# S5 input products with u as the weights, two groups side by side, and their results transposed back on TensorE

## The chip, the cores and the metric

The kernel runs on one core of a Trainium2 chip, in one launch. Its time is the device time of that core in microseconds, from the runtime; a profiled execution also gives a span, from the first to the last instruction. Five engines run their own instruction streams in order and wait for each other through semaphores: TensorE (PE; its weight loads are listed as PEld), VectorE (DVE), ScalarE (ACT), GpSimd (POOL) and SyncE (SP, which here only issues transfers). SBUF is the on-chip memory, PSUM the eight banks in which PE leaves its results, each 128 partitions of 512 float32.

## The reference

One encoder layer on 512 positions of 1024 features. The normalised input is projected once; the parts feed an S5 state-space branch, a gMLP branch and two gates; then come cross-attention on 256 memory tokens and a SwiGLU. What the change touches is the input side of the S5 scan:

```python
u = xa.astype(f32).reshape(bsz, seq, S5_GROUPS, S5_GROUP).transpose(1, 0, 2, 3)   # 32 groups of 16
lam_bar = jnp.exp(lam * step)
b_bar = ((lam_bar - 1.0) / lam)[..., None] * b
bu = jnp.einsum('gpc,lbgc->lbgp', b_bar, u.astype(jnp.complex64))     # 64 complex states a group
_, states = lax.associative_scan(_linear_recurrence, (a, bu), axis=0, reverse=reverse)
```

The scan runs in both directions over 512 positions.

## The kernel before

The kernel is one long program for the tile framework, whose scheduler sets the order of each engine's instructions, apart from those that the source pins with `in_order`. PE's main work is the layer's matrix products in three passes of float32r halves (`mm3`, L374): weights are loaded (`wraw`), split into `whi` by ACT (L85) and `wlo` by DVE (L86), and multiplied. `tokm` puts four token tiles in four PSUM banks (`pt`); `feat` takes two banks at a time (`pf`). Those banks come from a pool of five (`bank`, tag "mm"); a second pool of three banks (`aux`) serves transposes and small products.

The S5 branch is a generator beside that work. `tick` calls it after each block of products, and `later(n, f)` puts a step n blocks further down the program, so that its products stand between those of `pt` and `pf`. The positions are cut in 64 chunks of 8, and the scan goes over chunks. For each octet o of 8 groups (4 octets) and each of the real and the imaginary part i, so eight times:

- DVE forms 128x1024 coefficients in `wsx` (L972 to L976).
- `turn` transposes them on PE, four in each of two banks `pw` (L951), and ACT copies each bank to its half of the tile `wt` (L952).
- `apply` multiplies: for each group g, the weights are `wt[:, g]`, 128x128, the moving operand is `u[:, g]`, 64 chunks, and the result is 128 partitions (two directions of 64 states) by 64 chunks of the bank `pz` (L958).
- `keep` copies the lower half of the partitions on ACT (L963) and the upper one, reversed in time, on DVE (L964) to `zh`, which the scan (L985 to L988) goes over in place.

In the same stage ACT evacuates `pt` (L1089, `zt`), forms the squares of the gMLP's layer norm (L500, `squares`) from a mean `nm` that DVE made (L1134), normalises `zt` (L1142) with a root `r` from POOL (L1140), and from the first `pf` on evacuates gates (L1175, `gas`, with a table load ahead of the first). Much later, `s5_outputs` multiplies on the output side (L1014, `py`) with the same form that the change uses: weights `ss` or `u` of 64 columns, moving 128 columns, and two column halves j of PE in turn; then copies (`yn`, L1023) and transposes (`pyt`, L1029). For octets 2 and 3 the operand `tt` is loaded from POOL (L926) and the coefficients `e` are reloaded from SP.

Of the kernel before, what the change touches and what calls it, by code (L numbers as in the profile page):

```python
# [9 lines left out]
F32 = mybir.dt.float32  # L10
# [7 lines left out]
P = 128  # L18
# [22 lines left out]
NCH = T // Q  # L41
NO = 4
GO = G // NO
# [9 lines left out]
def hybrid_layer_kernel(  # L53
# [8 lines left out]
    nc = tc.nc  # L62
# [14 lines left out]
    def bank(name):  # L77
        return pm.tile([P, 512], F32, tag="mm", name=name)

    def aux(name, shape=(P, 512)):  # L80
        return pa.tile(list(shape), F32, tag="aux", name=name)
# [12 lines left out]
    in_order = tc.keep_in_program_order  # L94
# [362 lines left out]
    def later(n, fn):  # L457

        side["later"].append((side["now"] + n, fn))
# [30 lines left out]
    ident = cp.tile([P, P], F32, name="ident")  # L490
# [74 lines left out]
    s5p = s5.enter_context(tc.tile_pool(name="s5", bufs=1))  # L565
# [273 lines left out]
    def inner(t, gs, n):  # L839

        return t[:, gs, :].unsqueeze(3).to_broadcast([P, GO, t.shape[2], n])

    def outer(t, gs, n):

        return t[:, gs, :].unsqueeze(2).to_broadcast([P, GO, n, t.shape[2]])

    def lc(t, g):
        return t[:, g].rearrange("p a b -> p (a b)")
# [89 lines left out]
    def s5_inputs(o):  # L938

        gs = slice(o * GO, (o + 1) * GO)  # L940
        br, bi = st["b"]
        pr, pi = st["pw"]
        zh, u = st["zh"], st["u"]

        def turn(i, e):
            turned.add((o, i))
            wt = s5p.tile([P, GO, P], F32, tag="wt", name="wt", bufs=2)
            for hf in range(2):
                ps = aux("pw", (P, 4, P))
                for j in range(4):  # L950
                    nc.tensor.transpose(ps[:, j, :], lc(e, 4 * hf + j), ident)  # L951
                nc.scalar.copy(wt[:, 4 * hf:4 * hf + 4, :], ps)  # L952
            later(0.5, lambda: apply(i, wt))

        def apply(i, wt):
            ps = aux("pz", (P, GO, NCH))
            for g in range(GO):
                nc.tensor.matmul(ps[:, g, :], wt[:, g, :], u[:, o * GO + g, :], start=True, stop=True)  # L958
            zv = zh[:, :, i, gs].rearrange("p n g -> p g n")
            later(0.5, lambda: keep(zv, ps))  # L960

        def keep(zv, ps):
            nc.scalar.copy(zv[lo_], ps[lo_])  # L963
            V.tensor_copy(zv[hi_], ps[hi_, :, ::-1])  # L964
            st["nz"] = st.get("nz", 0) + 1

        for i in range(2):
            while o > 0 and (o - 1, i) not in turned:
                yield None
            e = wsx[:, 2 + i].rearrange("p g (c l) -> p g c l", c=C)  # L970
            w = s5p.tile([P, GO, C, Q], F32, tag="etmp", name="etmp2")
            V.tensor_tensor(e, inner(br, gs, Q), outer((pr, pi)[i], gs, C), ALU.mult)  # L972
            yield 1.1
            V.tensor_tensor(w, inner(bi, gs, Q), outer((pi, pr)[i], gs, C), ALU.mult)
            yield 1.1
            V.tensor_tensor(e, e, w, (ALU.subtract, ALU.add)[i])  # L976
            yield 1.1
            later(1, lambda i=i, e=e: turn(i, e))
# [134 lines left out]
    u = s5p.tile([P, G, NCH], F32, tag="u", name="u")  # L1113
# [74 lines left out]
    for h in range(H):  # L1188
        ps = bank("psv")
# [103 lines left out]
    for q, ts in ((5, T1), (6, T0)):  # L1293
        for i in range(2):
            k = slice(2 * i, 2 * i + 2)
# [308 lines left out]
    ps = {t: bank(f"pt{t}") for t in range(NT)}  # L1604
# [45 lines left out]
    held, ps = [], {}  # L1650
# [91 lines left out]
    ps = [bank("pf0"), bank("pf1")]  # L1742
# [247 lines left out]
```

## Time and profile before

| | us |
|---|---|
| median of 3 runs | 867.08 (866.55 to 867.7) |
| profiled execution | 867.03 |
| its span | 865.2 |
| PE busy in it | 856.6 |
| DVE busy | 660.4 |
| ACT busy | 466.1 |
| first and last start of the input products (L958) | 81.3 and 141.7 |

A row of an engine's timeline gives the start in the span, the length of a run of like instructions, the engine, the source line, the operation, out<-in, sizes and their number; in square brackets stands how long the engine was idle before it and who ended that. A float32 product leaves two MATMUL records, a float32 transpose or a float32r product one. A row of the waits names who waited, for whom, and gives the total in us, the number of times and the longest. A row of the stretches gives the bounds, the length, the busy time with the number of instructions of PE, PEld, DVE, ACT and POOL, the granted PE clock (1.00 is full), the busy share of the DMA engines and GB/s.

### The profile page before, as it was taken

To read this page: it belongs to the slowest core of one execution; us is meant where nothing else is said; L and a number is where in the kernel's file an instruction comes from. 1 tells how busy PE (TensorE), PEld (TensorE's weight loads), DVE (VectorE), ACT (ScalarE), POOL (GpSimd) and SP (SyncE) were. 2 spreads that over 40 slices of the span, in tenths; PEclk is the share of its full clock that TensorE was granted. 3 is DMA by queue.
4 is the path that set the end of the run, shared out by engine and by line. 5 is a ranking of instruction groups with operands and counts; after the bars stand their busy time and mean duration, and the time that the engine had idled before them with its cause. 6 is when DMAs were issued, how large, how long until landed. Compare 5 with 4: busy or idle time off the path is not lost.

```text
span 865.2 us, 14764 instructions
## 1 busy us (share of the span) xinstructions
PE 856.6 (99%) x5780; PEld 766.9 (89%) x5780; DVE 660.4 (76%) x1075; ACT 466.1 (54%) x698; POOL 91.6 (11%) x123
## 2 busy tenths in 40 slices
PE   9999999999999999999999999999999999999997
PEld 7888888888889988899899888999999999988875
DVE  7698997899846868678758756867877768899875
ACT  6734863244355544457547544645545555656564
POOL 0002302111021110110010001010211111000010
PEclk9999999999999999999999999999999999999999
DMA  8759565988574797735696555557899898366672
GB/s 271 192 173 308 110 178 153 252 194 193 145 220 152 242 316 246 238 106 200 210 278 159 144 150 142 146 162 193 206 227 240 217 236 214 96 186 205 197 237 102
DMA packets 115496, 169.56 MB, mean 196 GB/s; under 512 B 9297, under 2 KB 80481, under 8 KB 115298
## 3 DMA queue, kind: packets, MB, share of 16 engines
q1 hardware_dynamic: 94754, 138.50, 48.9%
q0 software_dynamic: 20384, 29.60, 20.5%
q8 instruction: 45, 0.74, 0.3%
q10 hardware_dynamic: 288, 0.52, 0.2%
q14 instruction: 25, 0.20, 0.1%
HBM read 159.71 MB, written 48.73 MB: 241 GB/s over the span
## 4 chain that ended last, share of the span: by engine, by line
PE 95%; DMA 1%; DVE 1%; ACT 1%; issue 1%; POOL 0%; SPq 0%; DVEq 0%; ACTq 0%; POOLq 0%
PE pf L374 27%; PE pt L374 17%; PE px L1238 13%; PE pq L1238 6%; PE dx L374 5%; PE dq L374 3%; PE pv L1238 3%; PE bx L1238 3%; PE qx L1238 3%; PE dv L374 2%; PE pz L958 2%; PE qv L1238 1%; PE po L374 1%; PE psc L374 1%; PE py L1014 1%; PE qq L1238 1%
## 5 line engine op out<-in xcount | busy, mean ns | idle before, releaser
L85 ACT CAST whi<-wraw 128x1024 fp32r<-128x1024 f32 x141 | 145.3, 1030 | 163.0 <-PE pf L374 55.5
L86 DVE TENSOR_TENSOR wlo<-wraw,whi 128x1024 fp32r<-128x1024 f32 x141 | 168.3, 1196 | 64.9 <-ACT whi L85 64.3
L374 PE MATMUL pf<-xn,whi 128*128 128x512 f32 x448 | 140.2, 393 | 0.0
L374 PEld LDWEIGHTS pf<-xn,whi 128*128 128x128 f32 x448 | 83.5, 188 | 16.8
L374 PE MATMUL pf<-xn,wlo 128*128 128x512 f32 x224 | 87.6, 391 | 0.0
L1238 PE MATMUL px<-fn,whi 128*128 128x256 f32 x480 | 83.4, 277 | 0.0
L1238 PEld LDWEIGHTS px<-fn,whi 128*128 128x128 f32 x480 | 72.5, 188 | 0.2
L86 DVE TENSOR_TENSOR wlo<-b,whi 128x1024 fp32r<-128x1024 f32 x40 | 48.9, 1224 | 26.0 <-ACT whi L85 26.0
L85 ACT CAST whi<-b 128x1024 fp32r<-128x1024 f32 x40 | 42.2, 1054 | 48.3 <-PE px L1238 27.8
L1238 PE MATMUL px<-fn,wlo 128*128 128x256 f32 x240 | 66.6, 277 | 0.0
L1238 PE MATMUL pq<-s,whi 128*128 128x256 f32 x320 | 55.0, 277 | 0.0
L374 PE MATMUL dx<-whi,s 128*128 128x512 f32 x166 | 52.2, 391 | 0.4 <-DVE h L1916 0.4
L86 DVE TENSOR_TENSOR wlo<-t,whi 128x1024 fp32r<-128x1024 f32 x30 | 36.7, 1225 | 18.4 <-ACT whi L85 18.4
L85 ACT CAST whi<-t 128x1024 fp32r<-128x1024 f32 x30 | 31.6, 1054 | 34.6 <-PE pv L1238 11.4
L374 PEld LDWEIGHTS pf<-xn,wlo 128*128 128x128 f32 x224 | 42.1, 188 | 8.6
L1238 PEld LDWEIGHTS pq<-s,whi 128*128 128x128 f32 x320 | 48.2, 188 | 0.0
L1238 PEld LDWEIGHTS px<-fn,wlo 128*128 128x128 f32 x240 | 45.2, 188 | 0.0
L1238 PE MATMUL pq<-s,wlo 128*128 128x256 f32 x160 | 44.3, 277 | 0.0
L374 PE MATMUL pt<-whi,xn 128*128 128x512 f32 x128 | 43.1, 403 | 0.0
L374 PEld LDWEIGHTS dx<-whi,s 128*128 128x128 f32 x166 | 31.1, 188 | 7.3 <-issue 0.8
L374 PE MATMUL dx<-wlo,s 128*128 128x512 f32 x83 | 32.3, 391 | 0.6 <-DVE wlo L86 0.6
L289 POOL DMA_DIRECT2D dsum<-in_w_down_dram x12 | 13.3, 1106 | 172.9 <-DMA dsum<-in_w_down_dram 169.2
(458 smaller groups left out, 2225.8 us busy)
## 6 DMA issues: line engine op xcount, KB each, us to landing
wraw<-in_w_in_dram SPq DMA_DIRECT2D x34, 512.0 KB, 4.0
dsum<-in_w_down_dram SPq DMA_DIRECT2D x20, 512.0 KB, 5.5
wraw<-dsum SPq DMA_DIRECT2D x20, 512.0 KB, 4.1
b<-in_w_gate_dram SPq DMA_DIRECT2D x15, 512.0 KB, 5.3
b<-in_w_up_dram SPq DMA_DIRECT2D x15, 512.0 KB, 4.6
wraw<-in_w_down_dram SPq DMA_DIRECT2D x15, 512.0 KB, 3.7
dsum<-in_w_down_dram POOLq DMA_DIRECT2D x10, 512.0 KB, 7.5
dsum<-dsum POOLq DMA_DIRECT2D x10, 512.0 KB, 7.7
```

The lines of the kernel that those rows point to most:

```text
L85: hi = nc.scalar.copy(dst_hi, src)
L86: lo = nc.vector.tensor_tensor(dst_lo, src, dst_hi.bitcast(F32), ALU.subtract)
L289: plan[j + step][1].append((0, lambda d=dst, x=more: nc.gpsimd.dma_start(d, x, accum_op=ALU.add)))
L374: m = nc.tensor.matmul(ps, a[x], b[y], start=start and i == 0, stop=stop and i == 2, skip_group_check=free)
L958: nc.tensor.matmul(ps[:, g, :], wt[:, g, :], u[:, o * GO + g, :], start=True, stop=True)
L1014: in_order(nc.tensor.matmul(ps[64 * j:64 * j + 64, :, :, h, :].rearrange("p q d c -> p d q c"), a, b, start=k == ks[0], stop=k == ks[2], t ...
L1238: nc.tensor.matmul(ps[:, j, :], a[x], b[y], start=start and j == k == i == 0, stop=k == 3 and i == 2, skip_group_check=True)
```

## The change

In `apply` operands change sides. `u[:, g]` (64 columns) is now the stationary weight and `wt[:, g]` (128 columns) moves. Groups 2k and 2k+1 go to the two 64-column halves of PE, so to partitions 0 to 63 and 64 to 127 of the same 128 columns of a bank; the eight products are pinned in that order. The result has chunks on partitions and states along the bank, so ACT copies the bank to `zr` in SBUF, which has one buffer (tag "y" of the pool "s5"), and four transposes of 128x128 bring it back to the layout of before in a bank `pzt`, from which `keep` copies as it did. The products' bank now comes from the pool of five, that of the transposes from the pool of three, where `pz` was before.

```diff
         def apply(i, wt):
-            ps = aux("pz", (P, GO, NCH))
-            for g in range(GO):
-                nc.tensor.matmul(ps[:, g, :], wt[:, g, :], u[:, o * GO + g, :], start=True, stop=True)
+            ps = bank("pz").rearrange("p (k n) -> p k n", k=4)
+            for k in range(4):
+                for j in range(2):
+                    g = 2 * k + j
+                    m = nc.tensor.matmul(ps[64 * j:64 * j + 64, k, :], u[:, o * GO + g, :], wt[:, g, :], start=True,
+                                         stop=True, tile_position=(0, 64 * j))
+                    if g:
+                        in_order(m)
+            zr = s5p.tile([P, 4, P], F32, tag="y", name="zr")
+            nc.scalar.copy(zr, ps)
+            ps = aux("pzt", (P, GO, NCH))
+            for k in range(4):
+                nc.tensor.transpose(ps[:, 2 * k:2 * k + 2, :].rearrange("p g n -> p (g n)"), zr[:, k, :], ident)
             zv = zh[:, :, i, gs].rearrange("p n g -> p g n")
             later(0.5, lambda: keep(zv, ps))
```

The scheduler orders the stage anew; source lines behind the change are 10 higher. The numbers behind names are those of the tile. PE's order where the second group's products stand (o = 0, i = 1), before:

```order
L374 MATMUL pf0_1040<-xn_137,whi_903 128x512
L374 MATMUL pf0_1040<-xn_138,whi_903 128x512
L374 MATMUL pf0_1040<-xn_137,wlo_904 128x512
L951 MATMUL pw_982<-ident_95,wsx_336 128x128 x4
L951 MATMUL pw_988<-ident_95,wsx_336 128x128 x4
L958 MATMUL pz_994<-u_549,wt_950 128x64 x8
```

The tile `wt_950` is copied from pw_951 and pw_957, which stand 25 products of `pt` and `pf` further up, directly behind pz_927. PE's order in the same place now, directly behind the last product of `pt`:

```order
L968 MATMUL pzt_938<-ident_95,zr_936 128x128 x4
L951 MATMUL pw_958<-ident_95,wsx_336 128x128 x4
L951 MATMUL pw_964<-ident_95,wsx_336 128x128 x4
L951 MATMUL pw_989<-ident_95,wsx_336 128x128 x4
L960 MATMUL pz_1001<-wt_957,u_549 64x128 x4
L951 MATMUL pw_995<-ident_95,wsx_336 128x128 x4
L960 MATMUL pz_1001<-wt_957,u_549 64x128 x4
L960 MATMUL pz_1033<-wt_988,u_549 64x128 x4
L374 MATMUL pf0_1061<-xn_137,whi_903 128x512
```

The transposes of two tiles and the products that use them have moved together, and pw_989 takes the PSUM bank of pw_958. ACT's order from the copy of the first group's result on, before:

```order
L963 COPY zh_835<-pz_927 64x8x64
L500 ACTIVATE squares_1032,ss_1088<-zt_334,nm_1087 128x512 x2
L952 COPY wt_950<-pw_951 128x512
L952 COPY wt_950<-pw_957 128x512
L500 ACTIVATE squares_1032,ss_1136<-zt_334,nm_1135 128x512 x2
L1089 ACTIVATE zt_334,zsum_335<-pt2_789 128x512
L85 COPY whi_910<-wraw_901 128x1024
L1089 ACTIVATE zt_334,zsum_335<-pt3_790 128x512
```

And now:

```order
L965 COPY zr_936<-pz_927 128x512
L500 ACTIVATE squares_1053,ss_1109<-zt_334,nm_1108 128x512 x2
L500 ACTIVATE squares_1053,ss_1157<-zt_334,nm_1156 128x512 x2
L1099 ACTIVATE zt_334,zsum_335<-pt2_789 128x512
L85 COPY whi_910<-wraw_901 128x1024
L1099 ACTIVATE zt_334,zsum_335<-pt3_790 128x512
L85 COPY whi_1065<-wraw_908 128x1024
L973 COPY zh_835<-pzt_938 64x8x64
L1152 ACTIVATE zt_334<-zt_334,nm_1108,r_1111 128x1024
L952 COPY wt_957<-pw_958 128x512
L952 COPY wt_957<-pw_964 128x512
```

The two `wt` copies stood behind three instructions of this stretch and now stand behind eleven. Further on, ACT's queue ahead of wt_1093, on which the products pz_1169 wait, is now:

```order
L1152 ACTIVATE zt_334<-zt_334,nm_1256,r_1259 128x1024
L1152 ACTIVATE zt_334<-zt_334,nm_1352,r_1355 128x1024
L85 COPY whi_1128<-wraw_1063 128x1024
L965 COPY zr_1042<-pz_1033 128x512
L973 COPY zh_835<-pzt_1012 64x8x64
L1185 ACT_TABLE_LOAD
L1185 ACTIVATE gas_1217<-pf0_1061 128x512
L85 COPY whi_1228<-wraw_1126 128x1024
L1185 ACTIVATE gas_1220<-pf1_1062 128x512
L973 COPY zh_835<-pzt_1044 64x8x64
L952 COPY wt_1093<-pw_1094 128x512
```

In the densest place (o = 2), PE's order was

```order
L951 MATMUL pw_1171<-ident_95,wsx_336 128x128 x4
L951 MATMUL pw_1177<-ident_95,wsx_336 128x128 x4
L958 MATMUL pz_1243<-u_549,wt_1157 128x64 x8
L374 MATMUL pf0_1195<-xn_137,whi_1107 128x512
L374 MATMUL pf0_1195<-xn_138,whi_1107 128x512
```

and is now

```order
L951 MATMUL pw_1199<-ident_95,wsx_336 128x128 x4
L960 MATMUL pz_1271<-wt_1185,u_549 64x128 x4
L951 MATMUL pw_1205<-ident_95,wsx_336 128x128 x4
L960 MATMUL pz_1271<-wt_1185,u_549 64x128 x4
L960 MATMUL pz_1287<-wt_1198,u_549 64x128 x8
L968 MATMUL pzt_1282<-ident_95,zr_1280 128x128 x4
L968 MATMUL pzt_1298<-ident_95,zr_1296 128x128 x4
L951 MATMUL pw_1304<-ident_95,wsx_336 128x128 x4
L951 MATMUL pw_1310<-ident_95,wsx_336 128x128 x4
L960 MATMUL pz_1369<-wt_1303,u_549 64x128 x4
```

Three groups' steps stand in a row without a product of `pf` between them; pw_1310 takes the bank of pw_1304.

## The prediction

> **What bounds the kernel now.** I read the page's busy shares and its chain first, then what TensorE (PE) waited for, then the stage that the change touches, 75 to 145 us into the span, engine by engine.
>
> ```profile
> span 865.2 us, 14764 instructions
> PE 856.6 (99%) x5780; PEld 766.9 (89%) x5780; DVE 660.4 (76%) x1075; ACT 466.1 (54%) x698; POOL 91.6 (11%) x123
> PE 95%; DMA 1%; DVE 1%; ACT 1%; issue 1%; POOL 0%; SPq 0%; DVEq 0%; ACTq 0%; POOLq 0%
> ```
> ```profile
> PE pt L573 <- DVE ones L493: 1.1, 1, 1.1
> PE dx L374 <- DVE wlo L86: 0.6, 1, 0.6
> ```
> ```profile
> 80.00:90.00 10.00, 10.00 (x59) 8.68 (x58) 9.94 (x15) 6.58 (x16) 2.35 (x2) 1.00 1.04 261
> ```
>
> PE is busy nearly throughout and carries 95% of the chain that ends last; the two longest entries of what it waited for are 1.1 and 0.6 us, at the two ends of the program. In the touched stage PE runs without a gap beside a VectorE (DVE) that is full as well (9.94 of 10 us). So time that PE is spared shows in the result one to one, and so does each new wait of PE. The profiled execution took 867.03 us, 1.8 outside its span; the median of the three runs is 867.08, so nothing has to be shifted.
>
> **The change on PE.** A group of eight input products, and the S5 output products, which already have the form that the change gives to the input products: 128x64 weights, 128 moving columns, two column halves in turn.
>
> ```profile
> 81.27 0.39 PE L374 MATMUL pt<-wlo,xn 128*128 128x512 f32 x1
> 81.50 1.89 PE L958 MATMUL pz<-u,wt 128*128 128x64 f32 x16
> 83.23 1.04 PE L951 MATMUL pw<-ident,wsx 128*128 128x128 f32 x8
> 84.03 0.71 PE L374 MATMUL pt<-whi,xn 128*128 128x512 f32 x2
> 84.57 0.40 PE L374 MATMUL pt<-wlo,xn 128*128 128x512 f32 x1
> 84.81 0.62 PE L374 MATMUL pt<-whi,xn 128*128 128x512 f32 x2
> 85.27 0.39 PE L374 MATMUL pt<-wlo,xn 128*128 128x512 f32 x1
> 89.12 0.62 PE L374 MATMUL pf<-xn,whi 128*128 128x512 f32 x2
> ```
> ```profile
> 240.38 0.39 PE L374 MATMUL pf<-xn,whi 128*128 128x512 f32 x1
> 240.70 0.66 PE L1014 MATMUL py<-e,ss 128*64 128x128 f32 x8
> 241.18 0.39 PE L1014 MATMUL py<-tt,u 128*64 128x128 f32 x4
> 241.40 0.61 PE L1014 MATMUL py<-e,ss 128*64 128x128 f32 x8
> 259.38 0.61 PE L1014 MATMUL py<-e,ss 128*64 128x128 f32 x8
> 259.92 0.39 PE L1238 MATMUL bx<-yb_hi,whi 128*128 128x256 f32 x1
> ```
>
> An operation's length overlaps the next one's; what it costs PE is the step from start to start. A float32 product leaves two records.
> - Removed: eight groups of 16 records, 83.23 - 81.50 = 1.73 us each: 13.8.
> - Added products: the same 16 records at the pace of py (241.40 - 241.18 = 0.22 for four, 0.055 each): 0.88 a group, 7.0 in all.
> - Added transposes: eight take 84.03 - 83.23 = 0.80, so 0.10 each; 32 of them: 3.2.
> - Going into and out of the 64-column form: 240.38 to 240.70 is 0.32 where a step of that row's form is 0.23 (81.27 to 81.50), so 0.09; at the other end eight records from 259.38 at 0.055 end at 259.82 and the next operation starts at 259.92, so 0.10. The order has the products in 12 unbroken pieces: 12 x 0.19 = 2.3.
> - The first float32r product behind float32 work: 84.03 to 84.57 is 0.54 against 0.46 (84.81 to 85.27). There are three more such returns: 0.25.
>
> Sum: -13.8 + 7.0 + 3.2 + 2.3 + 0.25 = -1.05, say -1.0 us. Bounds: without the piece costs -3.4; if the two halves did not run beside each other (then the pace of py would have to differ from its own row), +7 more.
>
> [...]
>
> **The change on ScalarE (ACT).** It gains a copy zr of 128x512 per group, and the two copies of pz (one on ACT, one on DVE) now wait for the transposes. ACT works strictly in its order, and the weight copies (wt from pw) that PE needs next stand behind these. Steps of ACT, start to start, and the DVE and POOL rows that feed it:
>
> ```profile
> 79.24 1.23 DVE L862 TENSOR_TENSOR e<-raw_c,pe 128x1024 f32<-128x1024 f32 x1 [1.96 <-DMA ed<-e]
> 85.00 0.15 DVE L1134 TENSOR_SCALAR nm<-nm 128x1 f32<-128x1 f32 x1
> 86.26 0.15 DVE L1134 TENSOR_SCALAR nm<-nm 128x1 f32<-128x1 f32 x1
> ```
> ```profile
> 85.18 0.72 ACT L500 ACTIVATE squares<-zt,nm 128x512 f32<-128x512 f32 x1 [0.67 <-DVE nm L1134]
> ...
> 85.90 0.71 ACT L500 ACTIVATE squares<-zt,nm 128x512 f32<-128x512 f32 x1
> ...
> 88.97 0.59 ACT L1089 ACTIVATE zt<-pt 128x512 f32<-128x512 f32 x1
> ...
> 89.54 1.04 ACT L85 CAST whi<-wraw 128x1024 fp32r<-128x1024 f32 x1
> 90.48 0.59 ACT L1089 ACTIVATE zt<-pt 128x512 f32<-128x512 f32 x1
> ...
> 93.82 1.24 ACT L1142 ACTIVATE zt<-zt,nm,r 128x1024 f32<-128x1024 f32 x1 [0.74 <-DVE nm L1141]
> 94.97 1.06 ACT L963 COPY zh<-pz 64x512 f32<-64x512 f32 x1
> ...
> 105.72 1.28 ACT L1175 ACT_TABLE_LOAD   x1
> 107.02 0.60 ACT L1175 ACTIVATE gas<-pf 128x512 f32<-128x512 f32 x1
> 107.51 1.04 ACT L85 CAST whi<-wraw 128x1024 fp32r<-128x1024 f32 x1
> ...
> 110.07 1.06 ACT L963 COPY zh<-pz 64x512 f32<-64x512 f32 x1
> 110.92 1.11 ACT L952 COPY wt<-pw 128x512 f32<-128x512 f32 x2
> ```
> ```profile
> 101.77 1.40 POOL L1140 TENSOR_TENSOR r<-ms,mhalf 128x1 f32<-128x1 f32 x1 [7.71 <-DVE ms L1139]
> ```
>
> Steps: squares 0.72, evacuation zt 0.57, cast 0.94, normalisation 1.15, zh 0.85, gate gas 0.49, table load 1.30. Two wt copies take 1.11, so a 128x512 copy about 0.6, with 0.5 to the next one.
>
> *First wait.* Until the first group nothing differs, so the clock of before holds. PE: products 81.50 + 0.09 + 0.88 = 82.47; then the 22 products of pt, which before took 84.03 to 89.12, 5.09: with the exit they end at 87.66; pzt and two pw, 12 transposes: 88.9. Next stands pw_989, whose PSUM bank is that of pw_958, so it waits for that tile's wt copy; behind it the products of pz need the same copy. ACT: zr 82.7; the squares need nm of DVE (85.00 and 86.26, whose order ahead of them is unchanged): 85.18, 85.90, 86.6, 87.3; evacuation 88.05; cast 88.6; evacuation of the last pt 89.55; cast 90.1; zh 91.05; normalisation 91.9; wt 93.05 to 93.65. PE starts pw_989 at 93.7 instead of 88.9: 4.8 us of waiting. Bounds: if DVE had not been held 1.96 us ahead of its row at 79.24, the squares would be done early and the chain would begin with the last evacuation at 87.9: end at 91.9, 3.0 of waiting; one microsecond more, 5.8, if a link is missed. I take 4.8, since the hold lies ahead of the change.
>
> *Second wait.* PE goes on from 93.7: transposes and half groups to 96.4, 14 products of pf, half a group, 12 products, pzt_1012, 22 products (5.09): pzt_1044 and two pw end at 110.0. pz_1169 then needs wt_1093. ACT: wt_988 to 96.4, four squares from 97.1 to 100.0, zr 100.0; both normalisations need an r from POOL, 1.40 each, the first not before DVE's sums at 100.9: normalisations 102.5 and 103.9, cast 105.05, zr 106.0, zh 106.5, table 107.35, gas 108.65, cast 109.15, gas 110.1, zh 110.6, wt 111.4 to 112.0. Wait: 2.0 us. Bounds: 0.8, if ACT is up to date when the second pf ends (gas, zh and wt still follow it), to 3.0.
>
> *Third wait.* Three groups are packed together. zr has one buffer, so the copy zr_1296 starts only when the transposes of zr_1280 are through: some 0.2 until the result is there (a record of 0.39 has a step of 0.23) and a copy of 0.6, while PE has nothing else in its order: 0.85. Then pw_1310 needs the bank of pw_1304, whose copy stands behind zr_1296 and two zh: 0.5 + 2 x 0.85 + 0.6 = 2.8 us from the start of zr_1296, of which PE fills 1.5 with that copy's wait and eight transposes: 1.3. With 0.2 for a wt copy just ahead, 2.3 us; bounds 1.5 and 3.0.
>
> *An earlier load wait.* Ahead of the third octet's output products, behind the second octet's transposes, the order has one product of pf where it had 21: 20 x 0.23 = 4.6 us earlier.
>
> ```profile
> tt<-kd POOLq DMA_DIRECT2D x8, 128.0 KB, 7.8
> ```
> ```profile
> 244.63 2.60 POOL L926 DMA_DIRECT2D tt<-kd  x4
> ```
> ```profile
> 257.15 0.44 PE L1014 MATMUL py<-tt,u 128*64 128x128 f32 x4
> ```
>
> Four loads issued 244.63 to 247.23 land 7.8 later, 252.4 to 255.0; at 257.15 that was hidden. At 252.6 each load arrives about as PE asks for it (every 0.66 us): 0 to 1.5, I take 0.5, since the first has 0.2 to spare only if its landing is the median.
>
> Everything else moves within slack: the later zh copies only feed a scan whose results PE first asks for at 240.70, and DMA issues on SP and POOL keep their number.
>
> **Sum.** -1.0 + 4.8 + 2.0 + 2.3 + 0.5 = +8.6 us on 867.03: 875.6.
>
> **The rivals.**
> 1. *The waits do not arise (other side).* Before, the same kinds of copies stood on ACT and PE never waited for one here. If the wt copies at the three places come in time, -1.0 is left, 866.0; with the piece costs hidden too, -3.4, 863.6. It decides once the waits together stay under 1.0 us. Against it: before, 22 and more products stood between a pw and its bank's next use; now none do. Chance 0.08, half of it for each figure.
> 2. *The waits shrink to their lower ends.* 3.0 + 0.8 + 1.5 + 0 - 1.0 = +4.3: 871.3. Chance 0.15.
> 3. *The clock falls in the first wait.*
>
> ```profile
> 861.00:865.00 4.00, 0.00 (x0) 0.00 (x0) 0.59 (x2) 0.44 (x1) 0.00 (x0) 0.89 0.37 144
> ```
>
> In the last 4 us of the span, without products, the granted clock averages 0.89: half speed for the last 0.9 us, so from about 864.1 on, more than 3 us into PE's idle time. A wait of 4.8 us could do the same; if PE then ran at half speed for as long as it had waited, 4.8 us, it would lose 2.4: 878.0. Against it: 4.8 is barely longer. Chance 0.22. [...]
> 4. *The halves do not run side by side*, +7: 882.6. py's rows speak against it. Chance 0.05.
>
> The forecast itself has 0.50. Range: from the shrunken waits to the clock's fall with a wait longer, 870.5 to 879.5; it leaves out rivals 1 and 4 and tails. Faster and slower mean by more than 0.2% (1.7 us), about what a measurement of this kernel can tell: faster 0.04, same 0.04, slower 0.92.
>
> **What would show it.** In the profile after: pz at 0.055 us a record, about 0.9 a group; PE's waits list with ACT wt as releaser, near 5 us at about 89 to 94, near 2 at about 110, and zr or wt for 2 in the densest place; PE's busy time about as before less one. I am wrong if ACT runs ahead of PE at pw_989, if the pieces cost more than 0.2 each, or if the clock leaves 1.00 behind the first wait.

## The result and the profile after

The changed kernel takes 878.13 us (median of 4 runs, 876.77 to 879.46) against 867.0 beside it on the same chip: ratio 1.0119, 95% interval 1.0101 to 1.0138, so 1.2% slower. The profiled execution took 877.96 us.

The changed kernel's page, in the lines that answer to those shown of before (span; busy time of each engine; shares of the chain that ended last), and then its list of what PE waited for (total, times, longest):

```profile
span 876.2 us, 14841 instructions
PE 859.9 (98%) x5812; PEld 764.2 (87%) x5812; DVE 660.9 (75%) x1075; ACT 470.7 (54%) x706; POOL 88.4 (10%) x123
PE 91%; DMA 3%; ACT 2%; DVE 2%; issue 1%; POOL 0%; SPq 0%; DVEq 0%; ACTq 0%; POOLq 0%
```
```profile
PE pw L951 <- ACT wt L952: 6.0, 2, 4.8
PE pz L960 <- ACT wt L952: 1.4, 1, 1.4
PE pzt L968 <- ACT zr L965: 0.7, 1, 0.7
```

The first three entries were not there before. They hold 8.2 of the 11.0 us by which the span grew: 4.82 + 1.19 for `pw`, 1.44 for `pz`, 0.73 for `pzt`. Three entries are four waits, and all lie in the touched stage. PE's timeline of the changed kernel at these waits, and ACT's beside the first of them:

```profile
87.97 0.60 PE L968 MATMUL pzt<-ident,zr 128*128 128x128 f32 x4
88.41 1.04 PE L951 MATMUL pw<-ident,wsx 128*128 128x128 f32 x8
94.26 1.11 PE L951 MATMUL pw<-ident,wsx 128*128 128x128 f32 x4 [4.82 <-ACT wt L952]
95.31 1.12 PE L960 MATMUL pz<-wt,u 128*64 128x128 f32 x8
96.36 1.12 PE L951 MATMUL pw<-ident,wsx 128*128 128x128 f32 x4
97.41 1.98 PE L960 MATMUL pz<-wt,u 128*64 128x128 f32 x16
99.31 1.07 PE L374 MATMUL pf<-xn,whi 128*128 128x512 f32 x2
...
114.89 0.66 PE L960 MATMUL pz<-wt,u 128*64 128x128 f32 x8 [1.44 <-ACT wt L952]
115.48 0.74 PE L374 MATMUL pf<-xn,whi 128*128 128x512 f32 x2
...
133.24 0.66 PE L968 MATMUL pzt<-ident,zr 128*128 128x128 f32 x4 [0.73 <-ACT zr L965]
...
135.53 0.66 PE L951 MATMUL pw<-ident,wsx 128*128 128x128 f32 x4 [1.19 <-ACT wt L952]
```
```profile
88.67 0.57 ACT L1099 ACTIVATE zt<-pt 128x512 f32<-128x512 f32 x1
...
89.24 1.03 ACT L85 CAST whi<-wraw 128x1024 fp32r<-128x1024 f32 x1
90.18 0.59 ACT L1099 ACTIVATE zt<-pt 128x512 f32<-128x512 f32 x1
...
90.76 1.03 ACT L85 CAST whi<-wraw 128x1024 fp32r<-128x1024 f32 x1
91.69 1.02 ACT L973 COPY zh<-pzt 64x512 f32<-64x512 f32 x1
92.53 1.22 ACT L1152 ACTIVATE zt<-zt,nm,r 128x1024 f32<-128x1024 f32 x1
93.65 1.04 ACT L952 COPY wt<-pw 128x512 f32<-128x512 f32 x2
```

The `pw` tile of 94.26 takes the bank of the first four records of 88.41; the copy that frees it is the first of the two in ACT's last row, behind two evacuations, two casts, a `zh` copy and a normalisation. ACT is never idle there: it is not overloaded on average (54%), it is in another order than PE needs.

The rows from 94.26 on show a second loss. Eight records of `pz` step 1.05 us (95.31 to 96.36) where the same eight step 0.59 at 114.89, and four transposes 1.05. The busy time in three stretches of 3.41 us of the changed kernel, with the granted clock in the third column from the end:

```profile
89.83:93.24 3.41, 0.00 (x0) 0.00 (x0) 2.94 (x4) 3.41 (x6) 0.08 (x1) 1.00 1.07 146
93.24:96.66 3.42, 2.40 (x14) 1.74 (x15) 3.36 (x6) 3.06 (x5) 0.00 (x0) 0.50 0.94 270
96.66:100.07 3.41, 3.41 (x22) 2.66 (x21) 3.38 (x7) 2.56 (x7) 0.00 (x0) 0.50 0.19 66
```

The clock is at half from 93.24 to 100.07. PE has work in 94.26 to 100.07 of that, 5.81 us; by the granted clock it loses half of it, an estimate of 2.9 us.

For all kernels the touched stage can be compared by itself, from the start of PE's first `pw` to the start of its last `psv` record; the PE operations in it are the same in every kernel but for what each edit says. It took 87.65 us before. In the table, the waits are those that PE's timeline names in the stage; the clock's loss is half of PE's time at half speed; idle products are the filler of two experiments; the rest is what remains, that is PE's own work against before. A piece is an unbroken run of the 64-column products, as in the prediction; how many an order has is counted in PE's timeline.

| kernel | stage against before | waits | clock | idle products | rest |
|---|---|---|---|---|---|
| changed | +11.92 | 8.18 | 2.91 | | +0.83 |
| e1_fill: idle products in the first wait | +8.70 | 2.86 | 0 | 4.35 | +1.49 |
| e2_late: the products later | +0.66 | 0 | 0 | | +0.66 |
| e3_products: the new products alone | -2.45 | 1.44 | 0 | | -3.89 |
| e4_ring: zr in two buffers | +9.90 | 5.79 | 3.09 | | +1.02 |
| e5_halves: the halves one behind the other | +14.73 | 8.19 | 2.97 | | +3.57 |
| e6_keep: the zh copies later | +10.77 | 8.03 | 1.71 | | +1.03 |
| e7_befcopy: before, with the copies | +0.97 | 0.52 | 0 | | +0.45 |
| e8_befturn: before, with copies and transposes | +8.45 | 3.60 | 0 | | +4.85 |
| e9_pools: other banks | -0.36 | 0 | 0 | | -0.36 |
| e10_fill_half: eight idle products | +9.88 | 5.08 | 1.66 | 2.08 | +1.06 |
| e11_late_whole: whole groups | +1.20 | 1.17 | 0 | | +0.03 |

### The profile page after: what moved, and what is told of

Its sections match the earlier page's. It is cut to its first block, busy times and chain, and to the rows that moved or that the text cites. A ratio compares the mean times of both kernels' runs of the same rounds, so it can differ in the third digit from the quotient of the medians.

```text
span 876.2 us, 14841 instructions
## 1 busy us (share of the span) xinstructions
PE 859.9 (98%) x5812; PEld 764.2 (87%) x5812; DVE 660.9 (75%) x1075; ACT 470.7 (54%) x706; POOL 88.4 (10%) x123
## 4 chain that ended last, share of the span: by engine, by line
PE 91%; DMA 3%; ACT 2%; DVE 2%; issue 1%; POOL 0%; SPq 0%; DVEq 0%; ACTq 0%; POOLq 0%
PE pf L374 26%; PE pt L374 14%; PE px L1248 12%; PE pq L1248 6%; PE dx L374 5%; PE dq L374 3%; PE pv L1248 3%; PE bx L1248 3%; PE qx L1248 2%; PE dv L374 2%; DMA ed<-e 1%; PE qv L1248 1%; PE po L374 1%; PE psc L374 1%; PE py L1024 1%; PE qq L1248 1%
```

## The experiments

The theory: PE's waits for ACT's weight copies, and a clock that falls because of the longest of them, make the time; PE's own work hardly changed. Against it stood that the added work is dear and the waits only show it, that ACT simply has too much to do, and that the fall of the clock has another cause.

### Idle products in the first wait

```diff
+                if (o, i, hf) == (1, 0, 0):
+                    for _ in range(18):
+                        in_order(nc.tensor.matmul(st["fill"], xn_hi[:, 0, :P], xn_hi[:, 0, :], start=True, stop=True))
                 for j in range(4):
-                    nc.tensor.transpose(ps[:, j, :], lc(e, 4 * hf + j), ident)
+                    m = nc.tensor.transpose(ps[:, j, :], lc(e, 4 * hf + j), ident)
+                    if (o, i) in ((0, 1), (1, 0)):
+                        in_order(m)
...
             nc.scalar.copy(zr, ps)
+            if (o, i) == (0, 0):
+                st["fill"] = ps.rearrange("p k n -> p (k n)")
```

> The changed kernel with 18 idle products (128x512, 0.23 us each, 4.1 us together) written into a bank whose contents have been copied out, ahead of the transposes that wait at 89 to 94 us. Theory (the clock falls because TensorE stands still for 4.8 us): the granted clock stays at 1.00 from 90 to 100 us, the wait there shrinks to under 1 us, its place is taken by the idle products, and the 2.9 us that half speed cost are gone: 875.2; as the order behind it shifts a little, the wait of 1.4 at 115 may go too, 873.8. Rival (the fall has another cause): the clock falls all the same, 878. Rival (there is no loss to the clock, the added work itself is dear): the clock stays and the time does too, 878.

Measured: 876.69 us, ratio 1.0087 (1.0072 to 1.0102). PE's timeline of this kernel:

```profile
89.17 4.35 PE L952 MATMUL pz<-xn 128*128 128x512 f32 x18
94.58 0.66 PE L954 MATMUL pw<-ident,wsx 128*128 128x128 f32 x4 [1.06 <-ACT wt L957]
95.17 0.66 PE L965 MATMUL pz<-wt,u 128*64 128x128 f32 x8
```

The same transposes start at 94.58, no earlier than without the idle products, and now take 0.59 instead of 1.05. The granted clock is 1.00 from 85 to 120 us. So the wait and the clock's fall are two losses, and the second went when PE stood still for 1.06 us instead of 4.82. The wait that PE had at 115 went too, as the order behind the filler shifted; the whole stage is 3.2 us shorter than in the changed kernel. By its ratio the kernel would take 874.5 beside a before of 867.0, between the two figures expected.

### The products later

```diff
-            later(0.5, lambda: apply(i, wt))
+            later(1.5, lambda: apply(i, wt))
```

> The changed kernel, the products of a group put 1.5 ticks behind its transposes instead of 0.5; every instruction is kept. Theory (TensorE waits for the weight copies because of the order on ScalarE): the three waits (4.8, 1.9 and 1.4 us) do not arise, the clock stays at 1.00, and what is left is the work, between -1.0 and 0 against before: 866.0 to 867.0, up to 2 more where later products make something else wait. Rival (the added work on TensorE is dear, the waits only show it): 874 or more. Rival (ScalarE has too much to do, whatever the order): waits of the same sum come back elsewhere, 873 or more.

Measured: 871.47 us, ratio 1.0033 (1.0022 to 1.0044). Not one of the four waits is left in the stage, the granted clock is 1.00 from 85 to 120 us, and the stage is 0.66 longer than before: the rivals, which wanted 873 or more, fall. The whole kernel is still 0.33%, 2.9 us, slower than before, more than expected. One new wait shows, in PE's list:

```profile
PE py L1024 <- DVE ss L1012: 1.0, 1, 1.0
```

The later products delay the scan, and the output products wait for it at 247 us. Against the trace of before another 2.6 us are lost between there and 335 us, where the output stage stands in another order; their cause stays open.

### The new products alone

```diff
-            zr = s5p.tile([P, 4, P], F32, tag="y", name="zr")
-            nc.scalar.copy(zr, ps)
-            ps = aux("pzt", (P, GO, NCH))
-            for k in range(4):
-                nc.tensor.transpose(ps[:, 2 * k:2 * k + 2, :].rearrange("p g n -> p (g n)"), zr[:, k, :], ident)
+            ps = ps.rearrange("p k (g n) -> p (k g) n", g=2)
```

> The new products alone: no copy zr, no transposes back; the two copies take the halves straight from the products' tile, so that the output is not the reference's. Theory (my prices): -13.8 + 7.0 for the products, 2.3 for the pieces, 0.25 for the returns, so TensorE's work is 4.2 less than before; without the copy in the chain the waits are under 2 us together and the clock stays: 862.8 to 864.8. Rival (the pieces or the products cost more than priced): 867 or more.

Measured: 866.44 us, ratio 0.9972 (0.9962 to 0.9983): by the ratio 2.4 us less than before. The stage is 2.45 shorter, with 1.44 of waits in it, so the products with their pieces save 3.9 us; 4.2 was priced, but for 12 pieces, and this kernel has 10. The step from its rest of -3.89 to kernels with everything in them (+0.66 with 12 pieces in e2_late, +0.03 and -0.36 with 9 in e11_late_whole and e9_pools), each put right by 0.2 to 0.3 for a piece more or less (the price comes from the last experiment), is what the transposes back and their returns cost: 3.7 to 4.2 us, not the 3.45 of the prediction.

### zr in two buffers

```diff
-            zr = s5p.tile([P, 4, P], F32, tag="y", name="zr")
+            zr = np_.tile([P, 4, P], F32, tag="ev", name="zr", bufs=2)
```

> The changed kernel, zr taken from the pair of buffers of the scratch tag ev instead of the single buffer of tag y. Theory: of the wait at 133 us the 0.7 us for the single buffer go, the first wait (4.8 us) and the fall of the clock behind it stay as they are; the wait of 1.4 at 115 may go as well, since the copies come in another order there: 875.5 to 877.4. Rival (the single buffer is what makes ScalarE late in all three places): the first wait goes with it and the time comes to about 868.

Measured: 876.56 us, ratio 1.0087 (1.0072 to 1.0102). The wait of `pzt` for `zr` (0.73) is gone, the one of 1.44 too; the first (4.57) and the fall of the clock (0.50 from 93.46 to 100.28) stay. The single buffer was one of the three places and not the cause of the first; the wait of 1.44 went with another order of the copies, which this run does not separate from the buffer.

### The halves one behind the other

```diff
-            for k in range(4):
-                for j in range(2):
+            for j in range(2):
+                for k in range(4):
```

> The changed kernel, the eight products of a group in another order: the four of the left column half first, then the four of the right one. The same instructions otherwise. Theory A (the two halves run beside each other, that is why a record costs 0.055 us): eight records in a row of one half cannot, each costs about 0.11, 0.88 more a group: 878 + 7 = 885. Theory B (0.055 us is what a record of this form costs by itself): nothing changes, 878.

Measured: 879.33 us, ratio 1.0136 (1.0121 to 1.0151). The first whole group, of the changed kernel and then of this one:

```profile
81.83 1.09 PE L960 MATMUL pz<-wt,u 128*64 128x128 f32 x16
82.85 0.73 PE L374 MATMUL pt<-whi,xn 128*128 128x512 f32 x2
```
```profile
81.45 1.58 PE L960 MATMUL pz<-wt,u 128*64 128x128 f32 x16
82.96 0.73 PE L374 MATMUL pt<-whi,xn 128*128 128x512 f32 x2
```

1.02 against 1.51 us. The order of the halves matters: taking turns is worth 0.49 a whole group; over the stage it is 2.7 (the rest of 3.57 against 0.83). Neither theory had the size: it is some 40% of the 7 us of theory A. The waits, 8.19 in all, are as they were.

### The zh copies later

```diff
-            later(0.5, lambda: keep(zv, ps))
+            later(1.5, lambda: keep(zv, ps))
```

> The changed kernel, the two copies into zh put 1.5 ticks behind the transposes instead of 0.5, so that one copy of 0.85 us no longer stands between the evacuations and the weight copies on ScalarE, and the transposes that wait come a little later. Theory (the fall of the clock follows from the length of the wait): the first wait is 2 to 3 us instead of 4.8, the clock stays at 1.00: 2 to 3 and another 2.9 less, 872.2 to 873.2, up to 2.6 more where the later copies delay something else. Rival (the fall comes at that place whatever the wait): the clock falls again, 875 to 878.

Measured: 879.96 us, ratio 1.0142 (1.0127 to 1.0157). The edit missed its aim: the first wait is 4.69 us, since the `zh` copy stayed ahead of the weight copies on ACT, and 2.5 us are lost later, in the output stage. Yet it says something of the clock. Busy time in the two stretches of 3.41 us around the fall:

```profile
90.84:94.25 3.41, 0.34 (x3) 0.34 (x4) 3.38 (x5) 3.41 (x6) 0.00 (x0) 1.00 1.15 225
94.26:97.66 3.40, 3.40 (x23) 2.41 (x23) 3.37 (x8) 2.47 (x5) 0.00 (x0) 0.50 0.71 224
```

A wait as long as the changed kernel's (4.69 and 4.82) cost 1.7 us at the clock and not 2.9: it was at 0.50 for 3.40 us here (94.26 to 97.66) and for 6.83 there (93.24 to 100.07). Here PE began again 0.34 us ahead of the fall, there 1.02 behind it. So two waits of nearly one length cost differently at the clock.

### Before, with one part each

```diff
                 nc.tensor.matmul(ps[:, g, :], wt[:, g, :], u[:, o * GO + g, :], start=True, stop=True)
+            zr = s5p.tile([P, GO, NCH], F32, tag="y", name="zr")
+            nc.scalar.copy(zr, ps)
```

> The kernel before with one part of the change: ScalarE also copies each group's products once more (128x512, eight copies), and nothing reads that copy. Theory (the waits come from what stands in a row, copy, transposes, copy, and from the few products that are left between a transposed tile and the next use of its bank): 867.0, no wait of TensorE in this stage. Rival (ScalarE has too much to do, 8 x 0.5 us is enough to make it late): waits of TensorE for wt, 869 or more.

Measured: 867.95 us, ratio 1.0007 (0.9997 to 1.0017), the same as before, with one wait of 0.52 in the stage, on DVE. Eight more copies on ACT cost nothing by themselves: the rival that ACT has too much to do falls.

```diff
+            zr = s5p.tile([P, GO, NCH], F32, tag="y", name="zr")
+            nc.scalar.copy(zr, ps)
+            ps = bank("pzt").rearrange("p (g n) -> p g n", g=GO)
+            for k in range(4):
+                nc.tensor.transpose(ps[:, 2 * k:2 * k + 2, :].rearrange("p g n -> p (g n)"), zr[:, 2 * k:2 * k + 2, :].rearrange("p g n -> p (g n)"), ident)
```

> The kernel before with the other part: the old products, then the copy zr and four transposes per group, from whose tile the two copies take zh; the values in zh are not the reference's then. [...] Rival (the waits come from the new products being faster): no waits, 870.5.

Measured: 875.36 us, ratio 1.0088 (1.0073 to 1.0103). Its waits in the stage come to 3.60 us, most of it in this entry:

```profile
PE pz L958 <- ACT wt L952: 2.7, 1, 2.7
```

With the row of copy, transposes and copy PE waits for a weight copy even at the old products; the granted clock is 1.00 from 85 to 120 us, with the longest wait, 2.72, in it. Without the waits the stage is 4.85 longer, for which the prediction had priced 3.45 (870.5 for the whole kernel): a second reading, beside the 3.7 to 4.2 above, that the transposes back are dearer than I had them, though here too the scheduler's order is another.

### Other banks

```diff
-                ps = aux("pw", (P, 4, P))
+                ps = bank("pw").rearrange("p (k n) -> p k n", k=4)
...
-            ps = bank("pz").rearrange("p (k n) -> p k n", k=4)
+            ps = aux("pz", (P, 4, P))
```

> The changed kernel with two tiles in other PSUM pools: the products' tile pz in the ring of three banks, as before the change, and the transposed weights' tile pw in the ring of five. Every instruction is kept. Theory (the waits come from which bank is used again and what stands ahead of its copy, so another ring takes them away as well as later products did): no wait over 1.5 us in this stage, the clock at 1.00, and the work left, which the kernel with the later products showed to be +0.6 in this stage: about 0.1 to 0.3% slower than before, 868 to 870. Rival (ScalarE cannot keep up with eight more copies in any order): waits of 3 us or more, 1.0% slower.

Measured: 868.08 us, ratio 1.0008 (0.9999 to 1.0017). With every instruction of the change kept and only two tiles in other rings, that is in the other pools of banks, the kernel is as fast as before. The scheduler's order changes with the rings, so the run does not tell the one from the other. ACT's timeline of this kernel, where the weight copies now stand between the squares instead of behind the evacuations, and PE's list of waits, in which nothing of the stage is left:

```profile
84.95 1.05 ACT L952 COPY wt<-pw 128x512 f32<-128x512 f32 x2
85.92 0.73 ACT L500 ACTIVATE squares<-zt,nm 128x512 f32<-128x512 f32 x1
...
87.35 0.57 ACT L952 COPY wt<-pw 128x512 f32<-128x512 f32 x1
87.81 0.59 ACT L1099 ACTIVATE zt<-pt 128x512 f32<-128x512 f32 x1
```
```profile
PE pt L573 <- DVE ones L493: 1.1, 1, 1.1
PE py L1024 <- DVE ss L1012: 1.0, 1, 1.0
PE dx L374 <- DVE h L1926: 0.4, 1, 0.4
```

The wait of `py` is that of the output products, as with the later products. The stage's rest is -0.36, the best of the kernels that compute everything: there the products stand in 9 pieces instead of 12. No kernel here that computes everything beat the one before.

### Eight idle products

The same edit as in the first experiment with `range(8)`. It asks whether the clock falls behind a shorter wait too, with a little work of PE in the 3.41 us ahead of the place.

> The changed kernel with 8 idle products (1.8 us) instead of 18 ahead of the waiting transposes, so that TensorE stands still for about 2.0 to 3.3 us there, less than the 3.41 us by which all clock changes in the records are spaced. [...]

Measured: 876.95 us, ratio 1.0111 (1.0097 to 1.0125). PE's timeline, and the busy time in two stretches, which end where the clock changes:

```profile
89.57 2.08 PE L952 MATMUL pz<-xn 128*128 128x512 f32 x8
94.84 1.12 PE L954 MATMUL pw<-ident,wsx 128*128 128x128 f32 x4 [3.19 <-ACT wt L957]
```
```profile
91.32:94.74 3.42, 0.33 (x2) 0.00 (x0) 3.39 (x5) 3.42 (x7) 0.00 (x0) 1.00 1.07 167
94.74:98.15 3.41, 3.31 (x18) 2.32 (x20) 2.24 (x5) 2.20 (x5) 0.00 (x0) 0.50 0.88 278
```

It does: with a wait of 3.19 us, and 0.33 us of work in the 3.42 ahead of the fall, the clock was at 0.50 for the next 3.41 us, and at 1.00 from 98.15 on.

### Whole groups

```diff
-            for k in range(4):
+            for k in (2, 3, 0, 1):
```

This stands on the kernel with the later products.

> The kernel with the products 1.5 ticks later, and in it the second half of each group's products ahead of the first, so that a group waits for both weight copies and is not cut in two by the transposes of the next tile: fewer pieces of the 64-column form. Theory (going into and out of that form costs 0.3 us a piece, not the 0.19 that I priced): three or four pieces fewer, 0.9 to 1.3 us less work in this stage, given back as far as the products now wait for the second copy (0 to 1.5): 0 to 0.1% less than with the later products alone, and the row of a piece shows the price. Rival (the extra work is the transposes): nothing changes in the work.

Measured: 871.1 us, ratio 1.0038 (1.0026 to 1.0051), the same as with the later products alone. The pieces went from 12 to 9 and the stage's rest from +0.66 to +0.03: 0.2 a piece, less than expected; a new wait of 1.17, `pzt` for `wt`, took more than that back in the stage. A piece's price by PE's timeline, of the changed kernel and, for transposes without a piece behind them, of the one before:

```profile
128.69 0.60 PE L951 MATMUL pw<-ident,wsx 128*128 128x128 f32 x4
129.22 0.66 PE L960 MATMUL pz<-wt,u 128*64 128x128 f32 x8
129.81 0.66 PE L951 MATMUL pw<-ident,wsx 128*128 128x128 f32 x4
```
```profile
120.00 0.60 PE L951 MATMUL pw<-ident,wsx 128*128 128x128 f32 x4
120.36 0.70 PE L374 MATMUL pf<-xn,whi 128*128 128x512 f32 x2
```

Four transposes step 0.53 ahead of a piece and 0.36 ahead of a product, so up to 0.17 to go in. But the product behind them then steps 0.53 (120.36 to 120.89) where 0.46 is usual, and ahead of more transposes four step 0.44 (87.97 to 88.41 in the changed kernel), by which it is 0.09. Eight records step 0.59 and would have 0.44, so 0.15 to come out. That makes 0.24 to 0.32 where transposes stand on both sides, and between 0.2 and 0.3 is as close as the runs bring it.

## Why the prediction was right, and where it was not

That the kernel gets slower, and by which mechanism, was right, and 878.1 lies in the range; but the likeliest case, 875.6, was 2.5 us short, and the time is that of the third rival. Two of the signs by which the prediction itself would be wrong came up: the clock left 1.00 behind the first wait, and a piece costs more than 0.2.

- *First wait.* 4.8 predicted, 4.82 measured, with the chain of ACT as laid out: the copy at 93.05 in the working, 93.65 in the trace; PE from 93.7, 94.26 in the trace. The first experiment and the one with other banks show that it is the copy's place that does it.
- *Second wait.* 2.0, measured 1.44 at 114.89, within its bounds.
- *Third wait.* 2.3 with 0.85 of it for the single buffer; measured 0.73 for that and 1.19 behind it, 1.92. The run with two buffers took the first part away.
- *Earlier load wait.* 0.5, did not occur; its bound of 0 held.
- *Work.* -1.0 predicted. With no waits at all (e2_late) it was +0.66 for the same 12 pieces. Two terms were too low: the step into and out of the 64-column form (0.19, by the runs 0.2 to 0.3), and the transposes back, 3.45 with their returns, by the runs 3.7 to 4.85. In a row transposes step 0.11 each (87.97 to 88.41 for four), 3.5 for the 32; what the rest of their price is stays open. The pace of the products, 0.055 us a record, held (the 24 records at 130.40 step 1.46, the eight at 129.22 0.59, so 0.87 for 16).
- *Rival 3, the clock.* This is the step that failed: "A wait of 4.8 us could do the same [...] Against it: 4.8 is barely longer", with a chance of 0.22. It fell in the profiled execution, after 3.8 us of idle time, and cost 2.9, where 2.4 was priced. The length of the wait was compared with the idle time after which the clock had fallen at the program's end ("more than 3 us"; by the trace PE ends at 859.65 and the clock falls at 864.15), as if the one gave a bound for the other. No run shows such a bound: the clock fell in the stage with waits of 3.19 (eight idle products), 4.57 (zr in two buffers) and 4.69 us (the zh copies later) too, and stayed at 1.00 with one of 2.72. By these runs a fall was the likely case for a wait of 4.8, and the forecast with it 878.
- *Sum.* 8.2 of waits, 2.9 of clock and 0.8 of work make the stage's 11.9. Behind the stage about 1 us comes back by the end of the span, most of it in the last 30 us, which the change doesn't touch. That rival 3's 878.0 and the measured 878.1 agree so closely is luck: 1.4 us of waits too many and that last 1 us make up for 1.9 of work and 0.5 of clock too few.
- *Rival 4, the halves.* The products kept py's pace of 0.055 us a record, so its condition does not hold; the order of the halves was worth 2.7 us, not 7.

## What to carry to other kernels

When an engine that sets the pace loses filler work between a producer and the next use of the same buffer, look at what stands ahead of the release on the other engine, in its order, not at that engine's share of busy time: eight more copies alone cost nothing, and the same copies with the tiles in other rings cost nothing either. A long wait of PE can have a second price, the time at half clock behind it: 2.9 us with the wait of 4.82 in the changed kernel, 1.7 with those of 4.69 and 3.19, and none with one of 2.72 (before, with copies and transposes). And an operand swap that halves a product's cost has to be summed with what it needs to put its result back: -3.9 here for the products alone, and between -0.4 and +0.7 with their results put back, waits left out.

## What the runs showed of the hardware

In the touched stage the granted clock was at 0.50 from 93.24 to 100.07 in the changed kernel, 6.83 us. With zr in two buffers that was 93.46 to 100.28, 6.82 us; with the zh copies later 94.26 to 97.66, 3.40; with eight idle products 94.74 to 98.15, 3.41. Stretches of that length, 3.41 us, are compared below. In the one ahead of the fall PE was busy for 0.00 us in the changed kernel, 0.34 with the later zh copies, 0.33 with eight idle products.

The kernel with 18 idle products, at its end, and the kernel with the halves apart have nearly the same work of PE in 3.41 us, 1.54 and 1.82. Behind the one the clock was at 0.50, behind the other at 1.00:

```profile
867.47:870.88 3.41, 1.54 (x13) 1.34 (x12) 1.90 (x6) 2.57 (x7) 0.00 (x0) 1.00 0.40 154
870.90:874.30 3.40, 0.00 (x0) 0.00 (x0) 0.06 (x1) 0.00 (x0) 0.00 (x0) 0.50 0.40 154
```
```profile
134.46:137.88 3.42, 1.82 (x13) 1.41 (x14) 3.35 (x4) 2.67 (x5) 1.16 (x1) 1.00 0.48 156
137.88:141.29 3.41, 3.41 (x17) 2.74 (x17) 3.31 (x4) 0.56 (x1) 0.00 (x0) 1.00 0.96 115
```

The wait of 2.72 us that left the clock at 1.00 (the kernel before with copies and transposes) lies across two stretches of 3.41 us, 95.12 to 98.53 and 98.53 to 101.94, with 1.90 and 2.12 us of work. The clock was still at 0.50 behind 2.40 us of work in 3.42 at half speed (the changed kernel at 93.24), and behind 2.77 in the kernel with zr in two buffers:

```profile
93.46:96.87 3.41, 2.77 (x15) 2.11 (x16) 3.35 (x6) 2.68 (x5) 0.00 (x0) 0.50 1.01 287
```

It was back at 1.00 behind 3.31 us of work in 3.41 (the kernel with eight idle products at 94.74) and behind 3.41 in 3.41 (the changed kernel at 96.66). By what the clock is set these rows do not show, and their busy times rest on the modelled ends of PE's operations.

The float32 transposes back of the changed kernel have 275 ns as the length of one record:

```profile
L968 PE MATMUL pzt<-ident,zr 128*128 128x128 f32 x32 | 4.9, 275 | 0.7 <-ACT zr L965 0.7
```

In a row they start 0.11 us apart (87.97 to 88.41 for four), so the length is not what one of them costs PE.
